# Two recurrent and attention layers with expert retrieval: candidate sums with a PSUM operand, a load buffer that lives longer, and a denser gather pace

## The chip, the cores and the metric

The kernel runs on one core of a Trainium2 chip. The metric is the device time of one execution in microseconds (us). Times of several runs are given as a median. A profiled execution gives the rows quoted below: what each engine did and what it waited for. The engines are PE (matrix products), DVE (vector), ACT (scalar functions), POOL (general work), and SP, which here only issues loads. Each engine runs its instructions in a fixed order.

## The reference

There are 512 tokens of width 1024 and two layers. Each layer is a mixer and an expert layer (PEER), both behind a modulated norm and both added back with a gate. The mixer of layer 0 is a gated linear recurrence (LRU, width 1408), that of layer 1 is causal attention with forget gates. The expert layer has 16384 experts, the pairs of 128 by 128 keys; each of 8 heads picks 16:

```python
def peer_ffn(h, q_w, subkey1, subkey2, expert_u, expert_v):
    ...
        q = (xc @ q_w).reshape(TOKEN_CHUNK, PEER_HEADS, 2, PEER_HALF)
        s1 = jnp.einsum('thd,hnd->thn', q[:, :, 0], subkey1)
        s2 = jnp.einsum('thd,hnd->thn', q[:, :, 1], subkey2)
        v1, i1 = lax.top_k(s1, PEER_TOPK)
        v2, i2 = lax.top_k(s2, PEER_TOPK)
        cand = (v1[..., :, None] + v2[..., None, :]).reshape(...)
        top_s, top_c = lax.top_k(cand, PEER_TOPK)
        ...
        g = jax.nn.softmax(top_s, axis=-1)
        u = jnp.take(expert_u, expert, axis=0)
        act = gelu(jnp.einsum('thkd,td->thk', u, xc))
        w = g * act
        return jnp.einsum('thk,thkd->td', w, jnp.take(expert_v, expert, axis=0))
```

The recurrence is

```python
def rglru_mixer(h, in_w, conv_w, conv_b, ra_w, ra_b, ri_w, ri_b, lam, out_w):
    xb, gb = split(h @ in_w)
    xb = causal_depthwise_conv(xb, conv_w, conv_b)
    r, i = sigmoid(blockdiag(xb, ra_w) + ra_b), sigmoid(blockdiag(xb, ri_w) + ri_b)
    log_a = -8 * softplus(-lam) * r
    u = sqrt(-expm1(2 * log_a)) * (i * xb)
    hs = scan(exp(log_a), u)
    return (hs * gelu(gb)) @ out_w
```

## The kernel before

**Weights.** Products in full precision are made from three products of split operands: high by high, low by high, high by low. A stream object holds all weight blocks in the order of their use. SP loads a block into a buffer `wraw`; ACT copies it to the rounded high half `whi` (line L189); the low half `wlo` = `wraw` - `whi` is made on DVE, or on POOL where `stream.on_pool` is set (L191). There are two load buffers. Where `stream.third` names a pool, every third load goes to a buffer of its own in that pool (L164 to L167), so that three loads can be on their way. A load can start only when the split of the block that was last in its buffer is done.

**Layer 0, in time.** The norm runs to about 46 us, the recurrence (`lru`) to 197, its output projection (`out_proj`, matrix products `oacc` at L599 to L601) to 266. In the recurrence the third buffer is in the pool `lw`, until the last block of input weights, when `third` becomes None. Pool `lw` closes at its end, so that the projection uses the pool `mw` for its third buffer in its first half, and none in its second. The results `yhi`, `ylo` of the recurrence lie in the pool `ly`, which lives to the end of the projection.

**Query stage of the expert layer** (`queries`, 290 to 470 us in layer 0, 1880 to 2060 in layer 1). For each of 8 heads and both halves of a query, PE projects the query into PSUM (`pacc`, L556 to L558), ACT takes the high half `qh` (L953), DVE the low half `ql` = `pacc` - `qh` (L954), and PE makes the scores `sps` against 128 keys (L941 to L943; the last of the three needs `ql`). DVE finds the 16 greatest of each set (`top16`: MAX8, its index, replacement, again), and puts them into `vals[0]` and `vals[1]`. After the first heads, `search` follows, one head behind: it adds the two sets to 50 candidates that can be among the 16 greatest sums, `cand`, by eight adds at L924 and one at L926, for all four blocks of 128 tokens at once, and takes their 16 greatest. In this stage POOL makes the `wlo` and the products `mq` (L264) of modulation matrices with a broadcast condition vector, whose sums ACT takes (L249). Between heads PE also makes the first inner products of the expert loop (`first_up`).

**Expert loop** (`expert_in`, `gated`, `expert_out`; 769 to 1480 us in layer 0, 2333 to 3064 in layer 1). Three of the four blocks of 128 tokens go through all experts, as dense products with gates of which most are zero. The loop runs over 128 chunks of 128 experts. Some chunks have their inner activations stored from an earlier stage ("stored"), the others make them here. DVE multiplies activations `at` by gates (L1331), and makes the low half `wl` (L1339) of the result `wh`, which PE needs for the products `vacc` (L1346). The fourth block of tokens goes another way: beside the loop, POOL gathers for each of its 128 (head, rank) pairs the rows of `expert_u`, later of `expert_v` (L1221), and DVE makes a product with the tokens (`rows`, L1234) and later a weighted sum (`accg`, L1248). These 256 steps are a background generator: in each chunk `pump` gives it a credit, by the two numbers of `PUMP`, the first for chunks that aren't stored, the second for stored ones; a step costs 1.2 of credit. What is left after the loop runs at once in `bg.finish()`.

The order of the instructions of each engine is set by a scheduler that works from its own costs, except for instructions that are pinned with `keep_in_program_order`, among them `wl` and the gathers' vector operations.

Of the kernel before, what the change touches and what calls it, by code (L numbers as in the profile page):

```python
# [6 lines left out]
F32 = mybir.dt.float32  # L7
# [5 lines left out]
AF = mybir.ActivationFunctionType  # L13
# [6 lines left out]
TC = S // 128  # L20
KD = D // 128
DR = 1408
NR = DR // 128
# [5 lines left out]
PH = 8  # L29
PK = 128  # L30
TOPK = 16
# [5 lines left out]
XT = 32  # L37
EARLY = (4, 0, 0, 2, 0, 2, 2, 2)
NEARLY = sum(EARLY)
PUMP = (4.05, 1.31)  # L40
QROWS = 6
LAG = 2
AHEAD = 6
# [633 lines left out]
def lru(g, h, head, conv, bias, lam, during, grow_fn, after):  # L677

    tc, nc = g.tc, g.nc
    V, A = nc.vector, nc.scalar  # L680
    with pool(tc, name="lruy", bufs=1) as ly:
        yhi = ly.tile([128, NR, S], F32R, name="yhi")
        ylo = ly.tile([128, NR, S], F32R, name="ylo")
        with pool(tc, name="lru", bufs=1) as lp, pool(tc, name="lruw", bufs=2) as lw:
            cv = lp.tile([128, NR, 5], F32, name="cv")
            nc.sync.dma_start(cv, conv)
            gb = lp.tile([128, 2, NR], F32, name="gbias")
            nc.sync.dma_start(gb, bias)
            lm = lp.tile([128, NR], F32, name="lm")
            nc.sync.dma_start(lm, lam)  # L690

            def small(name):
                return lp.tile([128, NR], F32, name=name)
            z = small("z")
            V.tensor_scalar(z, lm, -1.0, None, op0=OP.mult)
            az, th, u, u2, sp = small("az"), small("th"), small("u"), small("u2"), small("sp")
            den = small("den")
            A.activation(az, lm, AF.Abs)
            A.activation(th, az, AF.Tanh, scale=0.5)
            V.tensor_scalar(den, th, 3.0, None, op0=OP.add)  # L700
            V.reciprocal(den, den)
            V.tensor_scalar(u, th, -1.0, 1.0, op0=OP.mult, op1=OP.add)
            V.tensor_mul(u, u, den)
            atanh2(g, sp, u, u2)
            V.tensor_scalar(z, z, 0.0, None, op0=OP.max)
            V.tensor_add(sp, sp, z)
            sp2 = small("sp2")
            V.tensor_scalar(sp2, sp, 2.0, None, op0=OP.mult)
            sp4 = small("sp4")
            V.tensor_scalar(sp4, sp, -4.0, None, op0=OP.mult)  # L710
            V.tensor_scalar(gb, gb, 0.5, None, op0=OP.mult)

            psum = g.lps
            with pool(tc, name="lps2", bufs=2, space=PSUM) as psum2:
                g.stream.third = (lw,)
                bg = Background(*during(lw))
                ge = {}
                xc, xh, xl = {}, {}, {}

                def gates(chunks):  # L720


                    sg, T, m = {}, {}, {}
                    for o in chunks:
                        gh, gl = g.stream.take()
                        ins = [i for i in (o - 1, o, o + 1) if 0 <= i < NR]
                        for w in range(2):
                            ps = psum2.tile([128, S], F32, name=f"gps{w}", tag=f"gps{w}")
                            for i in ins:
                                b = i - o + 1  # L730
                                nc.tensor.matmul(ps, gh[:, w, b, :], xh[i], start=(i == ins[0]), stop=False)
                                nc.tensor.matmul(ps, gh[:, w, b, :], xl[i], start=False, stop=False)
                                nc.tensor.matmul(ps, gl[:, w, b, :], xh[i], start=False, stop=(i == ins[-1]))
                            sg[o, w] = lw.tile([128, S], F32, name=f"sg{w}", tag=f"sg{w}")
                            A.activation(sg[o, w], ps, AF.Tanh, scale=0.5, bias=gb[:, w, o:o + 1])
                    for o in chunks:
                        r = sg[o, 0]
                        T[o] = lw.tile([128, S], F32, name="T", tag="T")
                        A.activation(T[o], r, AF.Tanh, scale=sp2[:, o:o + 1], bias=sp2[:, o:o + 1])
                        A.activation(r, r, AF.Exp, scale=sp4[:, o:o + 1], bias=sp4[:, o:o + 1])  # L740
                    for o in chunks:
                        m[o] = lw.tile([128, S], F32, name="m", tag="m")
                        tc.keep_in_program_order(A.activation(m[o], T[o], AF.Sqrt, scale=0.25))
                    for o in chunks:
                        a, i_ = sg[o, 0], sg[o, 1]
                        V.scalar_tensor_tensor(m[o], a, 1.0, m[o], op0=OP.add, op1=OP.mult)
                        V.scalar_tensor_tensor(i_, i_, 1.0, xc[o], op0=OP.add, op1=OP.mult)
                        V.tensor_mul(m[o], m[o], i_)
                        hs = T[o]
                        V.tensor_tensor_scan(hs, a, m[o], 0.0, op0=OP.mult, op1=OP.add)  # L750
                        V.tensor_mul(hs, hs, ge[o])
                        split(g, yhi[:, o, :], ylo[:, o, :], hs)

                for j in range(NR):
                    if j == NR - 1:
                        g.stream.third = None
                    ps = head.pop(0) if head else proj_t(g, psum, h)
                    xp = lw.tile([128, S + 3], F32, name="xp", tag="xp")
                    V.memset(xp[:, 0:3], 0.0)
                    A.activation(xp[:, 3:], ps, AF.Copy)  # L760
                    xc[j] = lw.tile([128, S], F32, name="xc", tag="xc", bufs=4)
                    A.activation(xc[j], ps, AF.Identity, scale=cv[:, j, 3:4], bias=cv[:, j, 4:5])
                    for k in (2, 1, 0):
                        V.scalar_tensor_tensor(xc[j], xp[:, k:k + S], cv[:, j, k:k + 1], xc[j],
                                               op0=OP.mult, op1=OP.add)
                    xh[j] = lw.tile([128, S], F32R, name="xh", tag="xh", bufs=4)
                    xl[j] = lw.tile([128, S], F32R, name="xl", tag="xl", bufs=4)
                    split(g, xh[j], xl[j], xc[j])
                    bg.pump(LP)
                    ps = head.pop(0) if head else proj_t(g, psum, h)  # L770
                    ge[j] = lw.tile([128, S], F32, name="ge", tag="ge", bufs=3)
                    A.activation(ge[j], ps, AF.Gelu)
                    if j and j % 2 == 0:
                        gates((j - 2, j - 1))
                    if j == NR - 2:
                        grow = grow_fn(psum)
                    bg.pump(LP)
                bg.finish()
                gates((NR - 1,))
            g.lguard.__exit__(None, None, None)  # L780
        with pool(tc, name="mw", bufs=2) as mw, pool(tc, name="ops", bufs=1, space=PSUM) as psum:
            out_proj(g, psum, (yhi, ylo), NR, grow, Background(*after(mw)), mw)


def finish_mixer(g, y, nk, grow, after):
# [63 lines left out]
def peer(g, norm_fn, u, v, grow_fn, query_rows, nq, last_rows, nd, cost):  # L849
# [3 lines left out]
    V, A, T = nc.vector, nc.scalar, nc.tensor  # L853
# [6 lines left out]
    with pool(tc, name="pk", bufs=1) as pk:  # L860
# [32 lines left out]
        vals = [rs.tile([128, TC, PH, TOPK], F32, name=f"vals{w}") for w in range(2)]  # L893
# [9 lines left out]
        env = {}  # L903
# [13 lines left out]

        def search(hd):

            v1, v2 = vals[0][:, :, hd], vals[1][:, :, hd]  # L920
            cand = env["qw"].tile([128, TC, NCAND], F32, name="cand", tag="cand", bufs=1)
            for i in range(8):
                n = ROWN[i]
                V.tensor_tensor(cand[:, :, ROWO[i]:ROWO[i] + n], v2[:, :, 0:n],  # L924
                                v1[:, :, i:i + 1].to_broadcast([128, TC, n]), op=OP.add)
            V.tensor_tensor(cand[:, :, ROWO[8]:NCAND], v1[:, :, 8:16],  # L926
                            v2[:, :, 0:1].to_broadcast([128, TC, 8]), op=OP.add)
            for t in range(TC):
                top16(top[:, t, hd, :], pos[:, t, hd, :], cand[:, t, :], NCAND)

        def queries(pw, psum, banks):

            todo = []
            rows = itertools.chain(*query_rows(pw))
            due = 0.0

# [727 lines left out]
def model(tc, *aps):  # L1664
# [4 lines left out]
    with ExitStack() as ctx:  # L1669
# [39 lines left out]
        def flat(n):  # L1709
# [7 lines left out]
        peer(g, normed("l0_ffn"), flat("l0_u"), flat("l0_v"), grow("l0_ffn"),  # L1717
             lambda p: (queried("l0_ffn", p, gate), queried("l1_mix", p, every[AT:])), 30 / 15, None, 3, PUMP)
        fox(g, normed("l1_mix"), *arg("fox_", "fb", "qg", "kg"), lambda p: (mod("l1_ffn", p, first[M1:], 1),),
# [101 lines left out]
```

## Time and profile before

| what | us |
|---|---|
| median of three runs | 3087.73 (3086.15 to 3087.94) |
| profiled execution | 3084.97 |
| its span, first to last instruction | 3083.1 |
| PE busy | 2978.3 |
| DVE busy | 2621.3 |
| ACT busy | 1449.4 |
| POOL busy | 1188.9 |

The span is what the rows cover; the execution's own time is 1.9 us longer. A row of a timeline gives the start, the duration, the engine, the line of the code, the operation, output and inputs, shapes and a count, and in brackets how long the engine had sat idle and which instruction ended that. A row of a table of waits gives the waiting engine and line, whom it waited for, and then total us, number of waits, and the longest. A row of a table of windows gives the stretch, its length, busy us (and number of instructions) of the engines asked for, the granted clock of PE as a share of full speed, the busy share of the DMA engines, and GB/s. A row of a table of groups gives, behind the shapes and the count, busy us in total and the mean in ns.

### The profile page before, as it was taken

The numbers are of one execution on the slowest core, as the hardware profiler recorded it, in microseconds if no ns is written. First come the engines' busy times: TensorE is split into PE (matmuls) and PEld (weight loads), VectorE is DVE, ScalarE is ACT, GpSimd is POOL, SyncE is SP. The second block draws the span as 40 slices with busy tenths as digits, with TensorE's granted clock in tenths as the row PEclk, the third lists the DMA queues.
The fourth block names the chain that finished last, engine by engine and source line by source line (L and its number), as shares of the span: only waits on it lengthen the run. The fifth ranks groups of instructions, "written<-read, shape, count | busy, mean of one in ns | idle before, by whom it ended". The sixth has DMA issues, their size and how long they took to land.

```text
span 3083.1 us, 44436 instructions
## 1 busy us (share of the span) xinstructions
PE 2978.3 (97%) x16232; PEld 2616.2 (85%) x16232; DVE 2621.3 (85%) x4951; ACT 1449.4 (47%) x2284; POOL 1188.9 (39%) x906
## 2 busy tenths in 40 slices
PE   8999889999999999999999999899999999999998
PEld 6778679999888888888787778799999888888887
DVE  7866999997788889888869877989996888888888
ACT  6655445566333333333448844355564333333332
POOL 1002764110556555555211002542203755565552
PEclk9999889999999999999999999999999999999999
DMA  7445446798999999998542144358998999999996
GB/s 295 172 179 181 160 154 256 284 313 287 358 376 367 370 370 384 360 372 318 219 139 79 50 157 155 111 177 314 337 292 314 393 354 375 382 372 355 364 365 238
DMA packets 306844, 855.23 MB, mean 277 GB/s; under 512 B 26208, under 2 KB 161408, under 8 KB 267840
## 3 DMA queue, kind: packets, MB, share of 16 engines
q1 hardware_dynamic: 72464, 407.65, 34.7%
q0 software_dynamic: 93440, 336.11, 28.9%
q10 hardware_dynamic: 140720, 108.63, 10.8%
q8 instruction: 127, 2.08, 0.2%
q14 instruction: 93, 0.76, 0.1%
HBM read 767.93 MB, written 83.51 MB: 276 GB/s over the span
## 4 chain that ended last, share of the span: by engine, by line
PE 64%; DVE 21%; issue 7%; ACT 5%; DMA 3%; POOL 0%; DVEq 0%; SPq 0%; ACTq 0%; POOLq 0%
PE vacc L1346 25%; PE pacc L556 10%; PE pacc L558 10%; PE pacc L557 10%; DVE accg L1248 2%; DVE cand L924 2%; PE gps L1178 2%; ACT whi L189 2%; DVE wlo L191 2%; DVE pg L1205 1%; DVE tk L899 1%; DVE wl L1339 1%; DMA wraw<-in_l_vp_dram 1%; DVE idxs L898 1%; DVE idxs L901 1%
## 5 line engine op out<-in xcount | busy, mean ns | idle before, releaser
L189 ACT ACTIVATE whi<-wraw 128x1024 fp32r<-128x1024 f32 (+1 forms) x646 | 669.5, 1039 | 1023.6 <-PE vacc L1346 397.1
L191 DVE TENSOR_TENSOR wlo<-wraw,whi 128x1024 fp32r<-128x1024 f32 (+2 forms) x580 | 699.7, 1217 | 331.7 <-ACT whi L189 331.3
L556 PE MATMUL pacc<-hhi,whi 128*128 128x352 f32 (+1 forms) x2600 | 895.7, 345 | 0.0
L558 PE MATMUL pacc<-hhi,wlo 128*128 128x352 f32 (+1 forms) x2600 | 887.0, 341 | 1.7 <-DVE wlo L191 1.6
L557 PE MATMUL pacc<-hlo,whi 128*128 128x352 f32 (+1 forms) x2600 | 887.1, 341 | 0.0
L1346 PE MATMUL vacc<-whi,wh 128*128 128x512 f32 x1536 | 598.9, 390 | 0.0
L1346 PE MATMUL vacc<-wlo,wh 128*128 128x512 f32 x1536 | 597.9, 389 | 0.0
L1346 PE MATMUL vacc<-whi,wl 128*128 128x512 f32 x1536 | 553.8, 395 | 12.6 <-DVE wl L1339 11.7
L1221 POOL DMA_INDIRECT rows<-in_l_v_dram,ei x256 | 391.4, 1529 | 328.1 <-DVE accg L1248 278.2
L557 PEld LDWEIGHTS pacc<-hlo,whi 128*128 128x128 f32 x2600 | 495.3, 191 | 26.6
L556 PEld LDWEIGHTS pacc<-hhi,whi 128*128 128x128 f32 x2600 | 494.0, 190 | 27.2
L1221 POOL DMA_INDIRECT rows<-in_l_u_dram,ei x256 | 416.4, 1627 | 259.9 <-DVE rows L1234 196.1
L558 PEld LDWEIGHTS pacc<-hhi,wlo 128*128 128x128 f32 x2600 | 493.3, 190 | 27.0 <-DVE wlo L191 2.8
L1346 PEld LDWEIGHTS vacc<-whi,wl 128*128 128x128 f32 x1536 | 282.5, 188 | 91.5 <-DVE wl L1339 34.3
L1346 PEld LDWEIGHTS vacc<-whi,wh 128*128 128x128 f32 x1536 | 288.3, 188 | 57.1 <-ACT wh L1334 0.6
L1346 PEld LDWEIGHTS vacc<-wlo,wh 128*128 128x128 f32 x1536 | 288.7, 188 | 56.1
L1248 DVE SCALAR_TENSOR_TENSOR accg<-rows,act,accg 128x1024 f32<-128x1024 f32 x254 | 325.7, 1282 | 2.9
L1234 DVE SCALAR_TENSOR_TENSOR rows<-rows,hn 128x1024 f32<-128x1024 f32 x256 | 302.1, 1222 | 0.1
L1334 ACT ACTIVATE wh<-at 128x768 fp32r<-128x768 f32 x128 | 108.4, 847 | 240.2 <-DVE at L1331 235.4
L191 POOL TENSOR_TENSOR wlo<-wraw,whi 128x1024 fp32r<-128x1024 f32 (+1 forms) x62 | 125.2, 2027 | 139.3 <-ACT whi L189 139.2
L1083 POOL DMA_INDIRECT rowx<-in_l_u_dram,eix x36 | 61.0, 1695 | 242.5 <-DVE rowx L1101 153.4
L1331 DVE TENSOR_TENSOR at<-at,gtile 128x768 f32<-128x768 f32 x128 | 122.2, 954 | 0.0
(342 smaller groups left out, 3757.6 us busy)
## 6 DMA issues: line engine op xcount, KB each, us to landing
wraw<-in_l_uT_dram SPq DMA_DIRECT2D x128, 1024.0 KB, 8.0
wraw<-in_l_vp_dram SPq DMA_DIRECT2D x128, 1024.0 KB, 8.6
gscr<-st ACTq DMA_DIRECT2D x48, 1024.0 KB, 6.8
gtile<-gscr SPq DMA_DIRECT2D x90, 512.0 KB, 7.3
ascr<-at ACTq DMA_DIRECT2D x136, 176.0 KB, 4.7
at<-ascr ACTq DMA_DIRECT2D x68, 352.0 KB, 8.4
mw<-in_l_ffn_mw_dram POOLq DMA_DIRECT2D x32, 512.0 KB, 4.1
wraw<-in_l_qw_dram SPq DMA_DIRECT2D x16, 1024.0 KB, 4.8
```

The lines of the kernel that those rows point to most:

```text
L189: self.pin(nc.scalar.activation(hi, raw, AF.Copy))
L191: self.pin((nc.gpsimd if self.on_pool else nc.vector).tensor_sub(lo, raw, hi))
L556: nc.tensor.matmul(ps, whi[:, k, :], hhi[:, k, :n], start=(k == 0), stop=False))
L557: nc.tensor.matmul(ps, whi[:, k, :], hlo[:, k, :n], start=False, stop=False)
L558: nc.tensor.matmul(ps, wlo[:, k, :], hhi[:, k, :n], start=False, stop=(k == KD - 1))
L924: V.tensor_tensor(cand[:, :, ROWO[i]:ROWO[i] + n], v2[:, :, 0:n], v1[:, :, i:i + 1].to_broadcast([128, TC, n]), op=OP.add)
L1221: i = nc.gpsimd.indirect_dma_start(out=rows, out_offset=None, in_=src, in_offset=bass.IndirectOffsetOnAxis(ap=ei[:, j:j + 1], axis=0))
L1234: V.scalar_tensor_tensor(r, r, 1.0, hn, op0=OP.mult, op1=OP.mult, accum_out=act[:, j:j + 1]))
L1248: i = V.scalar_tensor_tensor(acc, r, w, acc, op0=OP.mult, op1=OP.add)
L1331: pin(V.tensor_tensor(shp, shp, gts[c // 8][:, :, c % 8:c % 8 + 2, :].rearrange("p b c t -> p c b t"), op=OP.mult))
L1334: (pin if c < 2 else lambda x: x)(A.activation(wh, at, AF.Copy))
L1346: T.matmul(acc[t][d], x[:, ts], y[:, d, :], start=(i == 0 and x is wh and y is vh), stop=(i == PK - 1 and x is wl))
```

## The change

Three edits. The pace numbers of the gathers rise by some 3%. In the recurrence the third load buffer is in pool `ly` and stays in use to its end and through the first half of the output projection. In `search`, ACT copies a head's `vals[0]` into a PSUM tile `v1`, which takes the bank of the tag "tp" (otherwise used for transposes), and the nine adds on DVE read that operand from there.

```diff
-PUMP = (4.05, 1.31)
+PUMP = (4.15, 1.35)
...
-                g.stream.third = (lw,)
+                g.stream.third = (ly,)
...
                 for j in range(NR):
-                    if j == NR - 1:
-                        g.stream.third = None
...
         with pool(tc, name="mw", bufs=2) as mw, pool(tc, name="ops", bufs=1, space=PSUM) as psum:
-            out_proj(g, psum, (yhi, ylo), NR, grow, Background(*after(mw)), mw)
+            out_proj(g, psum, (yhi, ylo), NR, grow, Background(*after(mw)), ly)
...
         def search(hd):
 
-            v1, v2 = vals[0][:, :, hd], vals[1][:, :, hd]
+            v2 = vals[1][:, :, hd]
+            v1 = env["v1"][:, :, hd * TOPK:(hd + 1) * TOPK]
+            A.activation(v1, vals[0][:, :, hd], AF.Copy)
             cand = env["qw"].tile([128, TC, NCAND], F32, name="cand", tag="cand", bufs=1)
             for i in range(8):
                 n = ROWN[i]
...
         def queries(pw, psum, banks):
 
             todo = []
+            env["v1"] = psum.tile([128, TC, PH * TOPK], F32, name="v1", tag="tp", bufs=1)
```

Lines from the search on move by one or two (L954 becomes L955, L1248 becomes L1249, L1339 becomes L1340; `top16` moves up by two).

DVE, layer 0, the sums of head 0, before (`vals_2603` is the first set, `vals_2604` the second; both are in SBUF):

```order
L899 MATCH_REPLACE tk<-vals_2604,sps 128x128
L924 TENSOR_TENSOR cand<-vals_2604,vals_2603 128x4x8
L924 TENSOR_TENSOR cand<-vals_2604,vals_2603 128x4x5
L900 MAX vals_2604<-tk 128x8
L924 TENSOR_TENSOR cand<-vals_2604,vals_2603 128x4x4
L924 TENSOR_TENSOR cand<-vals_2604,vals_2603 128x4x3
L901 MAX_INDEX idxs_2606<-vals_2604,tk 128x8
L924 TENSOR_TENSOR cand<-vals_2604,vals_2603 128x4x16
L924 TENSOR_TENSOR cand<-vals_2604,vals_2603 128x4x2 x3
L926 TENSOR_TENSOR cand<-vals_2603,vals_2604 128x4x8
```

The same place now (`v_2618` is the tile in PSUM):

```order
L898 MAX vals_2604<-tk 128x8
L899 MAX_INDEX idxs_2606<-vals_2604,tk 128x8
L924 TENSOR_TENSOR cand<-vals_2604,v_2618 128x4x16
L924 TENSOR_TENSOR cand<-vals_2604,v_2618 128x4x8
L924 TENSOR_TENSOR cand<-vals_2604,v_2618 128x4x5
L924 TENSOR_TENSOR cand<-vals_2604,v_2618 128x4x4
L924 TENSOR_TENSOR cand<-vals_2604,v_2618 128x4x3
L924 TENSOR_TENSOR cand<-vals_2604,v_2618 128x4x2 x3
L955 TENSOR_TENSOR ql<-pacc,qh 128x512
L926 TENSOR_TENSOR cand<-v_2618,vals_2604 128x4x8
```

The adds now stand together behind the last search of the second set, and the next `ql` has moved up between them. On ACT, the first copy stands just ahead of the high half of a block of query weights, in layer 0, where there was nothing between the rows around it:

```order
L249 ACTIVATE mq,qdot<-mq 128x1024
L253 ACTIVATE gate_l_ffn<-qdot,bias_l_ffn 128x1
L920 ACTIVATE v_2618<-vals_2603 128x4x16
L189 ACTIVATE whi<-wraw 128x1024
L954 ACTIVATE qh<-pacc 128x512
```

SP, the loads of the recurrence's output projection, before:

```order
L173 DMA wraw_1778<-in_lru_out_dram 128x2048
L173 DMA wraw_1860<-in_lru_out_dram 128x2048
L173 DMA wraw_1952<-in_lru_out_dram 128x1024
L173 DMA wraw_1982<-in_lru_out_dram 128x512
L173 DMA wraw_2046<-in_lru_out_dram 128x2048
L173 DMA wraw_2012<-in_lru_out_dram 128x2048
L173 DMA wraw_2152<-in_lru_out_dram 128x1024
```

and now:

```order
L173 DMA wraw_1778<-in_lru_out_dram 128x2048
L173 DMA wraw_1860<-in_lru_out_dram 128x2048
L173 DMA wraw_1952<-in_lru_out_dram 128x1024
L173 DMA wraw_1982<-in_lru_out_dram 128x512
L173 DMA wraw_2012<-in_lru_out_dram 128x2048
L173 DMA wraw_2046<-in_lru_out_dram 128x2048
L173 DMA wraw_2152<-in_lru_out_dram 128x1024
```

Blocks are used in the order of their numbers. The fifth, `wraw_2012`, was issued behind the sixth; now it stands ahead of it, and its buffer is the one of the second, `wraw_1860`.

DVE, the end of layer 1's expert loop, before:

```order
L1331 TENSOR_TENSOR at_29267<-at_29267,gtile 128x768
L1248 SCALAR_TENSOR_TENSOR accg<-rows,act,accg 128x1024
L191 TENSOR_TENSOR wlo<-wraw,whi 128x1024
L1248 SCALAR_TENSOR_TENSOR accg<-rows,act,accg 128x1024 x3
L1339 TENSOR_TENSOR wl<-at_29267,wh 128x768
L1331 TENSOR_TENSOR at_29339<-at_29339,gtile 128x768
L191 TENSOR_TENSOR wlo<-wraw,whi 128x1024
L1339 TENSOR_TENSOR wl<-at_29339,wh 128x768
```

and now:

```order
L1249 SCALAR_TENSOR_TENSOR accg<-rows,act,accg 128x1024 x2
L191 TENSOR_TENSOR wlo<-wraw,whi 128x1024
L1340 TENSOR_TENSOR wl<-at_29182,wh 128x768
L1332 TENSOR_TENSOR at_29303<-at_29303,gtile 128x768
L191 TENSOR_TENSOR wlo<-wraw,whi 128x1024 x2
L1340 TENSOR_TENSOR wl<-at_29303,wh 128x768
L1332 TENSOR_TENSOR at_29375<-at_29375,gtile 128x768
L1340 TENSOR_TENSOR wl<-at_29375,wh 128x768
```

The last gathered sums (`accg`) now come two pairs of chunks earlier.

## The prediction

> **What bounds the kernel now.** I read the page's busy shares first, then PE's waits stage by stage, and then the timelines of the engines named there.
>
> ```profile
> PE 2978.3 (97%) x16232; PEld 2616.2 (85%) x16232; DVE 2621.3 (85%) x4951; ACT 1449.4 (47%) x2284; POOL 1188.9 (39%) x906
> ```
>
> PE is busy for 97% of 3083.1 us, so about 105 us of idle time is all that shorter waits can return, and beside it the time in which PE ran at a lower granted clock. The change touches four stages. PE's waits in them are, in this order: the query stage of layer 0 (290 to 470 us) and of layer 1 (1880 to 2060), the LRU output projection (two rows, 197 to 270), the expert loop of layer 0 with its end (770 to 1520), the same loop without its end (770 to 1465), and the loop of layer 1 (2333 to 3083).
>
> ```profile
> PE sps L943 <- DVE ql L954: 28.8, 7, 9.8
> PE sps L943 <- DVE ql L954: 9.6, 4, 5.6
> PE oacc L599 <- ACT whi L189: 4.0, 1, 4.0
> PE oacc L600 <- DVE wlo L191: 0.5, 1, 0.5
> PE vacc L1346 <- DVE wl L1339: 6.3, 8, 3.1
> PE vacc L1346 <- DVE wl L1339: 2.4, 5, 1.3
> PE vacc L1346 <- DVE wl L1339: 5.5, 8, 3.1
> ```
>
> The query stage of layer 0 is the costliest: seven waits, 28.8 us, all for ql, the low half of a query, which DVE makes in order behind its search work.
>
> **Candidate sums.** These are the busy times of line L924's adds in the two query stages, then a window of all engines, then DVE's adds of one head (three rows), POOL's operations beside them (three rows), and one ql with the POOL operation that ran across it.
>
> ```profile
> 280.00:470.00 190.00, 53.37 (x56) 0.90 0.48 175
> 1880.00:2060.00 180.00, 19.96 (x64) 0.98 0.38 135
> 310.00:470.00 160.00, 131.16 (x656) 117.47 (x655) 151.53 (x731) 67.20 (x123) 113.69 (x94) 0.88 0.41 150
> ```
> ```profile
> 351.50 3.99 DVE L924 TENSOR_TENSOR cand<-vals,vals 128x32 f32<-128x32 f32 x2
> ...
> 355.61 2.25 DVE L924 TENSOR_TENSOR cand<-vals,vals 128x16 f32<-128x16 f32 x2
> ...
> 358.06 0.43 DVE L924 TENSOR_TENSOR cand<-vals,vals 128x64 f32<-128x64 f32 x4
> ```
> ```profile
> 348.40 2.40 POOL L191 TENSOR_TENSOR wlo<-wraw,whi 128x1024 fp32r<-128x1024 f32 x1 [0.71 <-ACT whi L189]
> 350.76 4.69 POOL L264 TENSOR_TENSOR mq<-mq,sc 128x1024 f32<-128x1024 f32 x2
> 355.40 2.34 POOL L191 TENSOR_TENSOR wlo<-wraw,whi 128x1024 fp32r<-128x1024 f32 x1
> ```
> ```profile
> 345.26 2.43 POOL L191 TENSOR_TENSOR wlo<-wraw,whi 128x1024 fp32r<-128x1024 f32 x1
> ...
> 346.50 0.67 DVE L954 TENSOR_TENSOR ql<-pacc,qh 128x512 fp32r<-128x512 f32 x1
> ```
>
> An add of 16 to 32 elements took up to two microseconds while POOL worked: the pair begun at 351.50 ended at 355.49 where POOL's pair ended (350.76 + 4.69 = 355.45), and the next pair ended at 357.86, where POOL's next operation ended at 357.74. With POOL idle four adds took 0.43 us. So an add with two SBUF operands waits out POOL's operations. The ql at 346.50 reads one operand from PSUM, lay wholly inside a POOL operation, and took 0.67 us. I take it that an add with one PSUM operand escapes in the same way.
>
> Eight free adds of L924 cost 2 x 0.43 = 0.86 us a head. Layer 0 pays 53.37 - 7 x 0.86 = 47.3 us too much on DVE (seven heads' adds fall into the window), layer 1 19.96 - 8 x 0.86 = 13.1 us. What PE gets back is less, since PE waits only in part of that time. In layer 0, between 310 and 470 us, PE idles 160 - 131.16 = 28.8 us, and in its busy time the mean granted clock was 0.88, so its work at the full clock is about 131.16 x 0.88 = 115.4 us. The upper end is therefore 160 - 115.4 = 44.6 us. POOL's 113.69 us and DVE's 151.53 - 47.3 = 104.2 us both fit under that time, but hardly: each is near PE, and POOL is as good as full. Those seven waits include two long ones:
>
> ```profile
> 360.58 0.47 PE L943 MATMUL sps<-whi,ql 128*128 128x128 f32 x1 [7.83 <-DVE ql L954]
> 410.87 0.48 PE L943 MATMUL sps<-whi,ql 128*128 128x128 f32 x1 [9.82 <-DVE ql L954]
> ```
>
> The lower end is these two alone, 17.7 us, with the shorter waits staying because POOL takes their place. I take 28, the idle time as such: the clock is then given back only where a new small wait doesn't take it again. In layer 1, PE's waits are 9.6 us and DVE's excess 13.1; the ends are 5.6 (the longest wait alone goes) and 13; I take 9.
>
> The copy to PSUM costs ACT eight instructions a layer. Nearest rows in this stage are a one-element ACTIVATE, and the wait that gives ACT room:
>
> ```profile
> L253 ACT ACTIVATE gate_l_ffn<-qdot,bias_l_ffn 128x1 f32<-128x1 f32 x8 | 2.3, 291 | 0.2
> ACT whi L189 <- PE pacc L557: 76.2, 23, 6.2
> ```
>
> At 0.3 us each that is 2.4 us a layer, under 76.2 us of ACT's idle time in layer 0: nothing on the path, and 2.4 us if that cover were gone. The copy waits for DVE's first set of top values and stands in ACT's order ahead of a whi; the adds come only after the second set, half a head later, so DVE should find it done. What DVE itself pays for a PSUM operand is bounded by two rows of the same operation and size, one reading PSUM (sps), one SBUF (tk):
>
> ```profile
> L897 DVE MAX8 vals<-sps 128x8 f32<-128x128 f32 x64 | 18.7, 291 | 7.1 <-PE sps L943 7.1
> L900 DVE MAX8 vals<-tk 128x8 f32<-128x128 f32 x63 | 17.7, 281 | 0.2
> ```
>
> The difference is 10 ns, or 9 x 8 x 0.01 = 0.7 us a layer on DVE, which I put at nothing, since DVE gains 47. The Trainium skill's "VectorE: DVE Perf Modes", in its section on the errata, speaks against the change here: it gives a DVE instruction 58 cycles of fixed cost with an SBUF source and 120 with a PSUM source, at 0.96 GHz. By it, my estimate is 62 cycles or 65 ns more for each add, 4.7 us of DVE time a layer, and some 4 us less gain in layer 0; the two rows above show 10 ns where it says 65, so I go by the rows.
>
> **Third weight buffer.** After the LRU's gates, its third load buffer was in a pool that closes; the fifth block of the output projection's weights used one of the next pool. Now the buffer lives on, and that load stands ahead of its neighbour in SP's order. Rows: DVE's split of the block three earlier, SP's issue, ACT's split of the block, and PE around it.
>
> ```profile
> 210.53 1.22 DVE L191 TENSOR_TENSOR wlo<-wraw,whi 128x1024 fp32r<-128x1024 f32 x1
> ```
> ```profile
> 218.25 0.81 SPq L173 DMA_DIRECT2D wraw<-in_lru_out_dram  x2
> ```
> ```profile
> 230.65 2.95 ACT L189 ACTIVATE whi<-wraw 128x1024 fp32r<-128x1024 f32 x3 [12.38 <-DMA wraw<-in_lru_out_dram]
> ```
> ```profile
> 227.34 0.40 PE L601 MATMUL oacc<-whi,ylo 128*128 128x512 f32 x1
> 231.76 0.80 PE L599 MATMUL oacc<-whi,yhi 128*128 128x512 f32 x1 [4.03 <-ACT whi L189]
> 233.02 0.80 PE L600 MATMUL oacc<-wlo,yhi 128*128 128x512 f32 x1 [0.47 <-DVE wlo L191]
> ...
> 238.10 0.39 PE L600 MATMUL oacc<-wlo,yhi 128*128 128x512 f32 x1
> ```
>
> The load was issued at 218.25, behind one that had to wait for its buffer, and landed just before 230.65, 12 us later. In the changed order it needs the buffer of the block three earlier, whose split ends at 211.75, and stands first: it lands by about 224 even if it takes 12 us again, ahead of PE's need at 227.7. Both waits go (4.0 and 0.5), and so does the slow clock behind them. From 227.34 to 238.10 PE issued 14 matmuls; at the pitch of 0.23 us in the full clock it needs 14 x 0.23 = 3.2 instead of 10.8. That is 7.5 us; the lower end is the 4.5 of the waits. I take 7. Earlier loads move up by one block too, and ACT meets the first output block's split ahead of the last gates' work, which can cost the LRU's tail up to 1.5 us; this stands in the range. The longer-lived buffer also makes three small loads at the LRU's start wait for earlier work, behind which PE has its first block of input weights: nothing, or about 1 us uncovered.
>
> **Gather pacing.** Each chunk of the loop now admits 4.15 instead of 4.05 (1.35 instead of 1.31 when stored) of gather work. By my count from the code 256 steps at 1.2 need 307.2; before, the loop admits about 305.2, and the rest falls to its very end, after about 313.2, so that the last gathers come some five steps earlier. DVE at the end of layer 1's loop, where accg is the gathers' sum and wl what PE waits for:
>
> ```profile
> 3059.35 3.92 DVE L1248 SCALAR_TENSOR_TENSOR accg<-rows,act,accg 128x1024 f32<-128x1024 f32 x3
> 3063.19 0.95 DVE L1339 TENSOR_TENSOR wl<-at,wh 128x768 fp32r<-128x768 f32 x1
> ```
> ```profile
> PE vacc L1346 <- DVE wl L1339: 3.8, 3, 3.1
> ```
>
> The second fence is PE's waits from 3030 us to the end, and the loop of layer 0 gives the same row from 1465 to 1520. In the changed order no accg stands between the last three wl, so these 3.8 us a layer go: 7.6 at most. Against it each chunk carries 2.5 to 3% more gather work, on DMA engines that are already full in parts of the loop:
>
> ```profile
> 1310.00:1340.00 30.00, 26.05 (x24) 1.00 1.01 412
> ```
>
> (stretch, its length, DVE busy, clock, DMA share, GB/s). The waits within the loops, 2.4 us in layer 0 and 5.5 - 3.8 = 1.7 in layer 1, could double: then the pacing is worth 7.6 - 4.1 = 3.5. As the lower end I put a stop of 0.1 us in each of 120 pairs of chunks (60 in a loop), 7.6 - 12 = -4.4. I take 6.
>
> **The sum.** 28 + 9 + 7 + 6 = 50 us off the profiled execution, whose time was 3084.97 us: 3035. The median of the runs, 3087.73, stands 2.8 above it, so the forecast against the median is 3037.7, which I give as 3038. The stages that follow each gain keep PE over 97% busy, so an earlier start carries through.
>
> **Rivals.** (1) POOL takes DVE's place in layer 0. For it: 113.69 us of work in a stage that would last 132, where the weight halves for PE queue behind pairs of mq operations.
>
> ```profile
> L264 POOL TENSOR_TENSOR mq<-mq,sc 128x1024 f32<-128x1024 f32 x27 | 64.0, 2395 | 0.0
> L191 POOL TENSOR_TENSOR wlo<-wraw,whi 128x1024 fp32r<-128x1024 f32 (+1 forms) x31 | 62.5, 2023 | 54.6 <-ACT whi L189 54.5
> ```
>
> If one mq of 2.4 us delays a wlo in each of eight heads, 19 of the 28 us are lost: gain 9 + 9 + 7 + 6 = 31, 3057. Against it: POOL today waits 54.5 us for ACT in that stage, so it runs ahead, and would have to lose all of that. (2) The adds are not freed by a PSUM operand: what lets ql through is something else. Then only 7 + 6 = 13 remain: 3075. The trace has no two-operand add of this small size from PSUM. (3) On the other side of no change: the copy blocks ACT. It waits for DVE's values and holds the whi behind it, and so POOL's wlo and PE. At head 0 the last of those values and that whi were these:
>
> ```profile
> 303.25 0.29 DVE L900 MAX8 vals<-tk 128x8 f32<-128x128 f32 x1
> 304.02 1.06 ACT L189 ACTIVATE whi<-wraw 128x1024 fp32r<-128x1024 f32 x1 [4.57 <-PE pacc L557]
> ```
>
> There were 0.5 us of slack. Where DVE is late, PE is then late through both ql and whi. It decides against the change from 50/16 = 3.1 us lost for each of 16 heads; at 5 us (a whole set of top values) it is 80 lost against 50: 3118. Against it: DVE loses 60 us of work and so is seldom late. (4) The pacing stops PE in the loops, at its lower end: 28 + 9 + 7 - 4.4 = 39.6, 3048.
>
> **Chances.** Forecast 0.63, with a range of its own from 3024 to 3050; POOL 0.18; adds not freed 0.08; copy blocks ACT 0.05; pacing 0.06. All ends at their best give 44.6 + 13 + 7.5 + 7.6 = 72.7, 3015; all at their worst 17.7 + 5.6 + 4.5 - 1.5 - 4.4 = 21.9, 3066. I start the range at 3019 and end it at 3064, past POOL's case, which leaves out the second and third rivals (0.13) and little below. A measurement tells some 0.2%, 6 us, from no change. Slower by more: rival three, 0.04. Within: part of two and three, 0.03. Faster: 0.93.
>
> **What would show it.** Right: the adds in layer 0's query stage together near 7 us instead of 53, with POOL busy beside them; PE's wait for ql there under 8 us; POOL's own waits for ACT well under 54; no wait for whi in the LRU's output projection and a clock of 1.00 through it; no wait for wl in the last three pairs of chunks of either loop. Wrong: adds that still end where POOL's operations end; PE waiting for wlo from POOL, or ACT's copy waiting while a whi stands behind it; more than 5 us of waits for wl inside a loop. The prediction as a whole fails if the query stage of layer 0 keeps its length.

## The result, and the profile after

The changed kernel took 3040.52 us in the median of four runs (3037.91 to 3042.44), the kernel before 3087.84 (four runs, the three given above among them): a ratio of 0.9845, 95% interval 0.9828 to 0.9862. The forecast was 3038, range 3019 to 3064. The profiled execution's span is 3040.4 us.

First the page's busy shares, then PE's waits by stage. Stages now begin earlier, and lines have moved by one: query stage of layer 0 (280 to 470 us) and of layer 1 (1840 to 2030), output projection (197 to 270), expert loop of layer 0 with its end (740 to 1500) and of layer 1 (2290 to 3043).

```profile
PE 2964.9 (98%) x16232; PEld 2605.4 (86%) x16232; DVE 2563.0 (84%) x4951; ACT 1451.8 (48%) x2300; POOL 1157.9 (38%) x906
```
```profile
PE sps L944 <- DVE ql L955: 0.7, 1, 0.7
PE sps L944 <- DVE ql L955: 0.7, 1, 0.7
PE oacc L600 <- DVE wlo L191: 0.7, 1, 0.7
PE vacc L1347 <- DVE wl L1340: 10.4, 6, 3.0
PE vacc L1347 <- DVE wl L1340: 10.9, 7, 2.7
```

The waits for ql have gone (28.8 and 9.6 before), those of the output projection are down from 4.5 to 0.7, but the waits for wl in the loops have risen, from 6.3 to 10.4 and from 5.5 to 10.9.

Where the 43 us came from is read off the first matrix products of the stages, in the two profiled executions. Each length is from the first row of one output on PE to the first of the next (the last loop: to its last product):

| stage | before | changed | difference |
|---|---|---|---|
| to the output projection | 196.8 | 198.5 | +1.7 |
| output projection | 69.1 | 62.6 | -6.5 |
| first scores to the next stage, layer 0 | 195.7 | 153.1 | -42.6 |
| expert loop, layer 0 | 745.4 | 753.6 | +8.2 |
| first scores to the next stage, layer 1 | 165.3 | 153.2 | -12.1 |
| expert loop, layer 1 | 744.9 | 753.7 | +8.8 |
| all other stages together | 961.0 | 960.7 | -0.3 |

**Sums.** The busy times of L924 in the two query stages, and the window of all engines in layer 0's stage (PE, PE's weight loads, DVE, ACT, POOL, clock, DMA):

```profile
270.00:440.00 170.00, 6.39 (x64) 1.00 0.63 226
1840.00:2000.00 160.00, 6.38 (x64) 1.00 0.41 145
```
```profile
306.50:432.00 125.50, 124.80 (x706) 112.96 (x706) 112.24 (x790) 73.35 (x136) 113.09 (x100) 1.00 0.57 207
```

The adds take 6.4 us in place of 53.4 and 20.0. PE is busy for 124.80 of 125.50 us, at the full clock, where it was busy for 131.16 of 160 at 0.88. POOL's 113.09 us of work fit into it with little to spare. DVE's adds of head 0, and POOL at the same time:

```profile
306.50 0.76 DVE L924 TENSOR_TENSOR cand<-vals,v 128x64 f32<-128x64 f32 x8
```
```profile
302.67 4.75 POOL L264 TENSOR_TENSOR mq<-mq,sc 128x1024 f32<-128x1024 f32 x2
307.38 3.11 POOL L191 TENSOR_TENSOR wlo<-wraw,whi 128x1024 fp32r<-128x1024 f32 x2
```

Eight adds ran in 0.76 us, wholly inside POOL's pair of operations, which ended only at 307.42. Of the 72 adds of a layer none took more than 0.21 us. The price of the PSUM operand is read from the ninth add, L926, in the views of the tile cand, of before and of the changed kernel (minimum, median, maximum in ns):

```profile
L926 DVE TENSOR_TENSOR cand<-vals,vals x7: 178/179/184, 320.2 to 454.1; 128x32 f32<-128x32 f32 x7
```
```profile
L926 DVE TENSOR_TENSOR cand<-v,vals x8: 179/183/185, 307.8 to 427.9; 128x32 f32<-128x32 f32 x8
```

That is 4 ns, not the 65 worked out from the errata table of the Trainium skill's page "VectorE: DVE Perf Modes".

**Load.** SP issued the fifth block at 213.72 us, where it had been 218.63 (the second issue of the row that begins at 218.25), and PE's window over the place of the old stop is full, at the full clock (before: 10.51 of 15 us and 0.87 from 220 to 235):

```profile
222.00:237.00 15.00, 15.00 (x65) 1.00 0.61 217
```

**Loops.** The stop at the loop's end has gone, and stops inside have come. DVE ahead of one of them, in the changed kernel, and at the same place before:

```profile
1240.41 3.92 DVE L1249 SCALAR_TENSOR_TENSOR accg<-rows,act,accg 128x1024 f32<-128x1024 f32 x3
1244.24 1.22 DVE L191 TENSOR_TENSOR wlo<-wraw,whi 128x1024 fp32r<-128x1024 f32 x1
1245.38 1.32 DVE L1249 SCALAR_TENSOR_TENSOR accg<-rows,act,accg 128x1024 f32<-128x1024 f32 x1
1246.62 0.94 DVE L1340 TENSOR_TENSOR wl<-at,wh 128x768 fp32r<-128x768 f32 x1
```
```profile
1287.64 3.92 DVE L1248 SCALAR_TENSOR_TENSOR accg<-rows,act,accg 128x1024 f32<-128x1024 f32 x3
1291.48 0.95 DVE L1339 TENSOR_TENSOR wl<-at,wh 128x768 fp32r<-128x768 f32 x1
```

One more sum (1.3 us) and a low half of a weight (1.2) now stand ahead of wl, and PE, which had waited 0.37 us here (the last row below, of before), waits 3.02 and then runs slowly:

```profile
1247.62 1.84 PE L1347 MATMUL vacc<-whi,wl 128*128 128x512 f32 x6 [3.02 <-DVE wl L1340]
1249.25 0.63 PE L1347 MATMUL vacc<-whi,wh 128*128 128x512 f32 x1
```
```profile
1292.48 1.65 PE L1346 MATMUL vacc<-whi,wl 128*128 128x512 f32 x6 [0.37 <-DVE wl L1339]
```

In the changed kernel, stops of 2.7 to 3.0 us stand at 1247.6, 1357.7 and 1443.4 us, and at 2808.2, 2918.3 and 3003.8. Behind each of these six some products ran at 0.63 us in place of 0.39, which cost about 1.5 us more a stop. So of the 17 us that the two loops lost, about 10 are longer waits (21.3 us for wl over the span, 11.7 before), and the slow products make up the rest.

### The profile page after: what moved, and what is told of

It reads as the page before. It is cut to its first block, busy times and chain, and to the rows that moved or that the text cites. A ratio compares the mean times of both kernels' runs of the same rounds, so it can differ in the third digit from the quotient of the medians.

```text
span 3040.4 us, 44431 instructions
## 1 busy us (share of the span) xinstructions
PE 2964.9 (98%) x16232; PEld 2605.4 (86%) x16232; DVE 2563.0 (84%) x4951; ACT 1451.8 (48%) x2300; POOL 1157.9 (38%) x906
## 4 chain that ended last, share of the span: by engine, by line
PE 69%; DVE 16%; issue 8%; ACT 4%; DMA 2%; POOL 1%; DVEq 0%; ACTq 0%; SPq 0%; POOLq 0%
PE vacc L1347 27%; PE pacc L556 11%; PE pacc L557 10%; PE pacc L558 10%; DVE accg L1249 2%; PE gps L1179 2%; DVE wlo L191 2%; ACT whi L189 1%; DVE pg L1206 1%; DVE rows L1235 1%; DVE wl L1340 1%; PE oacc L600 1%; PE oacc L599 1%; PE oacc L601 1%; DMA wraw<-in_l_uT_dram 1%
## 5 line engine op out<-in xcount | busy, mean ns | idle before, releaser
L1347 PE MATMUL vacc<-whi,wl 128*128 128x512 f32 x1536 | 564.3, 399 | 22.0 <-DVE wl L1340 21.3
L1222 POOL DMA_INDIRECT rows<-in_l_v_dram,ei x256 | 369.6, 1444 | 348.0 <-DVE accg L1249 275.2
L1222 POOL DMA_INDIRECT rows<-in_l_u_dram,ei x256 | 409.3, 1599 | 242.7 <-DVE rows L1235 179.3
L1249 DVE SCALAR_TENSOR_TENSOR accg<-rows,act,accg 128x1024 f32<-128x1024 f32 x254 | 326.3, 1285 | 3.1
L1340 DVE TENSOR_TENSOR wl<-at,wh 128x768 fp32r<-128x768 f32 x128 | 121.8, 951 | 1.8 <-ACT wh L1335 1.8
```

The costliest lines, as they stand in the source:

```text
L1222: i = nc.gpsimd.indirect_dma_start(out=rows, out_offset=None, in_=src, in_offset=bass.IndirectOffsetOnAxis(ap=ei[:, j:j + 1], axis=0))
L1249: i = V.scalar_tensor_tensor(acc, r, w, acc, op0=OP.mult, op1=OP.add)
L1340: return lambda: pin(V.tensor_sub(wl, at, wh))
L1347: T.matmul(acc[t][d], x[:, ts], y[:, d, :], start=(i == 0 and x is wh and y is vh), stop=(i == PK - 1 and x is wl))
```

## The experiments

Three questions: does each part do what the stages say; is it the PSUM operand that frees the sums; and why does a denser pace cost time. On the last, theory P says that position matters. Two chunks that share one wl are called a pair here. From the two pace numbers the steps can be counted that `pump` admits in each chunk. PE makes inner products for some of the later chunks; at the pairs 7, 16, 25, 34, 43, 52 and 59 of the loop it makes none for two pairs running, so it needs the next wl soonest there. Ahead of that wl stand the last steps of the pair before and the first of this one: by the old pace 1 + 3 at all seven, by the new one 1 + 4 at 43, 52 and 59, which are the three stops. At 25 and 34 it has 2 + 3, also five, with no stop at 25 and 0.24 us at 34: the four in the last chunk before the wl are what hurts. Rival D says that density matters: more gather work at a time overloads DVE or the DMA engines.

**The old pace, with sums and load buffer as changed**

```diff
-PUMP = (4.15, 1.35)
+PUMP = (4.05, 1.31)
```

> The change with the old pace numbers (4.05, 1.31): sums from PSUM and the longer-lived load buffer alone. Theory P (the new pace costs time, because it puts one more gather step ahead of a low half wl where PE is shortest): both expert loops return to their old length, 745 us instead of 754, so the time is about 3040.5 - 17 = 3024. Rival T (the loops are longer because they now start earlier or in another phase, not because of the pace): the loops stay at 754 and the time at 3040.

Measured: 3028.48 us, ratio 0.9817 (0.9799 to 0.9835). The loops took 749.5 and 744.9 us; the profile's span was 3023.4. PE's waits over the whole span, with the stops of 3.1 us back at both ends:

```profile
PE vacc L1347 <- DVE wl L1340: 13.1, 17, 3.1
```

So the new pace cost about 12 us in the median. By the two ratios it is 9 us, with intervals that overlap a little (0.9828 to 0.9862 and 0.9799 to 0.9835), so this pair of runs alone would not settle it; the run of the pace alone, below, does. The loop of layer 0 was 4 us longer than before for two reasons. It had three waits of 0.9 to 1.3 us in its first half, where the kernel before had one of 1.3. And behind the stop of 3.08 us at its end the products ran at 0.63 us, which cost some 2.6 us, where in the kernel before they ran at 0.39 behind the same stop.

**The sums alone** (the kernel before with only the copy and the adds as changed)

> The kernel before with the PSUM operand of the sums alone. Layer 0's query stage, from its first scores to the next stage, should shorten by 42 to 43 us and layer 1's by 12, as in the changed kernel's trace, so 3088 - 55 = 3033; my prediction's sizes of 28 and 9 would give 3051. PE's wait for wl should be as before, 3 us at each loop's end.

Measured: 3036.47 us, ratio 0.9842 (0.9824 to 0.9859); query stages 153.1 and 153.2 us, as in the changed kernel. The output projection keeps its stop and its length (69.9 us):

```profile
PE oacc L599 <- ACT whi L189: 4.4, 1, 4.4
```

**The pace alone** (the kernel before with `PUMP = (4.15, 1.35)`)

> The kernel before with the new pace numbers alone. Theory P: each loop gains its 3.1 us stop at the end and loses three stops of 2.7 to 3 us with slow clock behind each, +8 us a loop, 3104. My prediction's step: 6 us less, 3082. Rival T (an interaction with the earlier start): no change, 3088.

Measured: 3100.86 us, ratio 1.0055 (1.0035 to 1.0075). The loops took 754.2 and 750.4 us; PE waited for wl, over the whole span,

```profile
PE vacc L1346 <- DVE wl L1339: 20.6, 14, 2.7
```

where it had waited 11.7 us before, with three stops of 2.7 us in each loop. The earlier start isn't needed for it: the pace alone makes the kernel slower. The loop of layer 1 lost 3 to 4 us less than that of layer 0 because two of its stops had no slow products behind them:

```profile
2865.36 1.65 PE L1346 MATMUL vacc<-whi,wl 128*128 128x512 f32 x6 [2.74 <-DVE wl L1339]
2866.85 0.39 PE L1346 MATMUL vacc<-whi,wh 128*128 128x512 f32 x1
```

**Load buffer alone**

> The kernel before with the longer-lived load buffer alone. The output projection goes from 69 to 62.5 us, as in the changed kernel, and 3088 becomes 3081. If the recurrence pays for the buffer, its end moves from 196.8 to 198.5 us and 3083 is left; the runs without this edit, whose recurrence ended at 198.0 and 198.8, speak against that.

Measured: 3080.56 us, ratio 0.9984 (0.9973 to 0.9996); the output projection took 61.6 us. The recurrence ended at 198.8 us, but so it did in the run of the pace alone, without this edit. The +1.7 us of the table above is therefore no measure of the buffer's cost: the recurrence ended between 196.8 and 198.8 us in the four traces without the edit and between 197.6 and 199.1 in the eight with it. A cost of about a microsecond can't be excluded.

**ACT's copy into SBUF instead of PSUM**

```diff
-            env["v1"] = psum.tile([128, TC, PH * TOPK], F32, name="v1", tag="tp", bufs=1)
+            env["v1"] = pw.tile([128, TC, PH * TOPK], F32, name="v1", tag="v1", bufs=1)
```

> As the run with the old pace, but ACT's copy of the first set of values goes to a tile in SBUF instead of PSUM: same instructions, both operands of the sums in SBUF. Theory S (what frees the sums is that one operand is in PSUM): the sums in layer 0's query stage take some 50 us again, the stage goes from 153 back to 190 to 196 us, layer 1's from 153 to 165, and the time from 3028 to 3080. Rival R (the order of DVE, or the fresh copy, freed them): sums at 7 us, 3028.

Measured: 3104.83 us, ratio 1.0053 (1.0036 to 1.007), with the load buffer's gain in it. L924's busy time in the query stages, and the longest waits of PE (whole span) and of ACT (280 to 480 us):

```profile
280.00:480.00 200.00, 64.23 (x64) 0.88 0.46 164
1840.00:2100.00 260.00, 27.34 (x64) 0.94 0.40 145
```
```profile
PE sps L944 <- DVE ql L955: 52.0, 10, 13.0
```
```profile
ACT v L920 <- DVE vals L898: 63.9, 6, 15.6
```

The sums are long again with the same copy, so the fresh copy isn't what freed them. DVE's order changed in this run too: the adds stand between the searches again, as in the kernel before. So this run alone doesn't part the operand's place from the order; the next one does. The stages took 205.5 and 175.9 us, 10 longer than before the change. Where DVE is late, the copy waits in ACT's queue (63.9 us, against 24.8 in the changed kernel), with the high halves of PE's weights behind it: the mechanism of my third rival. That it makes the 10 us wasn't tested apart.

**POOL's products narrow, in the kernel before**

```diff
-        pin(P.tensor_tensor(wf, wf, g.sc, op=OP.mult))
+        pin(P.tensor_tensor(wf[:, :64], wf[:, :64], g.sc[:, :64], op=OP.mult))
```

> The kernel before, with POOL's products mq done for 64 of 1024 columns only (the modulation loses the rest): these POOL operations fall from 2.4 us to about 0.2, and half of POOL's work in layer 0's query stage goes. Theory S (the sums wait for whatever POOL operation with two SBUF operands is under way): the sums go from 53 us to about 25, what the weight halves on POOL block, the stage from 196 to about 165 and the time to about 3055. Rival R (the sums are long for a reason of their own): 53 us and 3088.

Measured: 3044.41 us, ratio 0.9854 (0.984 to 0.987). The sums, with both operands in SBUF, in the two stages:

```profile
280.00:480.00 200.00, 14.01 (x64) 0.98 0.60 216
1840.00:2100.00 260.00, 7.96 (x64) 0.98 0.56 207
```

From 53.4 us (56 adds) to 14.0 (64 adds), with DVE's instructions in the same order as in the kernel before: the sums had waited for POOL, and the order isn't what made them long. Together with the run before it this leaves the operand's place as what frees them. The adds that are still long end where one of POOL's `wlo` operations ends. That the total is less than the 25 expected may mean that the pairs of mq did most of the blocking, or only that POOL now has gaps, so that fewer adds meet one of its operations; the run doesn't part these. The stages took 157.9 and 155.7 us.

**Same credit as the new pace, steps placed otherwise**

```diff
-PUMP = (4.05, 1.31)
+PUMP = (4.12, 1.39)
```

> Sums and load buffer as changed, pace (4.12, 1.39): in sum the same credit as the new pace (320 against 319 over a loop) but such that before no low half wl of the pairs of chunks 25, 34, 43, 52 and 59, where PE is short, more than four gathered steps fall. Theory P (position): no stop of 2.7 us in the loops and none of 3 us at their end, loops of about 741 us, 3040.5 - 24 = 3017. Rival D (density: more gather work at a time costs DVE or the DMA engines): loops of 754 again, 3040.

Measured: 3017.57 us, ratio 0.9775 (0.9756 to 0.9795); loops of 743.4 and 740.9 us. The stops at the loops' ends are gone and none of 2.7 us has come. PE's wait for wl over the whole span, the longest of 1.9 us:

```profile
PE vacc L1347 <- DVE wl L1340: 5.7, 13, 1.9
```

Before that one of 1.9 us DVE had itself waited 1.3 and 0.5 us for gathered rows. Another execution of the same kernel (below, 739.9 and 740.0 us) has no wait for wl over 0.4 us. A late row can thus make a single stop that another execution doesn't have.

**More credit still, placed so too**

```diff
-PUMP = (4.05, 1.31)
+PUMP = (4.35, 1.32)
```

> Sums and load buffer as changed, pace (4.35, 1.32): more credit than the new pace (328 against 319 over a loop), again with no more than four gathered steps before the wl of the pairs where PE is short. Theory P (position): loops of 741 to 743 us, 3016, as with (4.12, 1.39). Rival D (density): worse than (4.12, 1.39) by some us a loop, 3025 or more.

Measured: 3017.64 us, ratio 0.977 (0.9753 to 0.9786); loops of 741.6 and 741.8 us. Some 3% more credit than the changed kernel's pace cost nothing where the steps lie well.

**One hundredth, placed badly** (beside the fastest version on the same chip)

```diff
-PUMP = (4.05, 1.31)
+PUMP = (4.05, 1.32)
```

> Sums and load buffer as changed, pace (4.05, 1.32): one hundredth on the second number of the old pace, credit 311.3 against 310.6 over a loop, but by the count of steps five instead of four fall before the wl of the pairs 7 to 59 where PE is short. Theory P (position): stops of 2.7 to 3 us at pairs 43, 52 and 59, with slow clock behind each, in both loops, as with the pace (4.15, 1.35), while the stop of 3.1 us at the end shrinks; loops of 752 to 756 us and 3040. Rival D (density): loops of 745 to 748, 3028.

> The fastest version beside the one before it on the same chip: 3017 to 3018 again, and ahead of the pace (4.05, 1.32) by 22 us by theory P, by 10 or less by rival D.

Measured: 3056.67 us (ratio 0.9896, 0.9878 to 0.9914) against 3015.35 (0.9767, 0.9751 to 0.9784). The loops took 763.1 and 758.8 us, against 739.9 and 740.0:

```profile
PE vacc L1347 <- DVE wl L1340: 33.5, 19, 4.0
```

With 1 + 4 steps at all seven pairs there are seven stops of over a microsecond in layer 0's loop, 106 to 110 us apart but for the last (821.9, 930.2, 1036.9, 1145.3, 1255.4, 1365.4 and 1452.0), of 1.1 to 4.0 us, and seven in layer 1's. The kernel was 41 us behind the fastest version, where theory P had said 22 and rival D 10 or less. The loss was larger than theory P's own figure, at least in part because it named three stops of the seven. That position makes these stops is shown: with a credit of 311 for a loop they come, with 320 and 328 they don't, so density isn't their cause over this range.

Over all twelve traces the loops fall into groups by pace: 744.9 to 749.5 us by the old one (12 loops), 750.4 to 754.2 by the new one (4), 739.9 to 743.4 by the two that place the steps well (6), and 758.8 and 763.1 by (4.05, 1.32).

## Why the prediction was right, point by point

The time fell into the range, 2.5 us from the forecast, but by two errors that cancelled: the sums gave 18 us more than forecast, and the pacing 23 less. That the forecast came so close is luck; its mechanisms for the sums and the load buffer were right, that for the pacing was wrong.

- **Sums, layer 0: mechanism right, size too small.** "I take 28, the idle time as such: the clock is then given back only where a new small wait doesn't take it again." Measured: 42.6, near the upper end of 44.6. The waits fell to 0.7 us, so no small wait took the clock again, and it was 1.00 all through. Both experiments on the mechanism (copy in SBUF, narrow products) bear out its step "an add with two SBUF operands waits out POOL's operations".
- **POOL's own waits for ACT** fell from 54.5 to 9.0 us in layer 0's query stage, as the prediction asked.
- **Sums, layer 1:** 9 taken, 12.1 measured, within the ends of 5.6 and 13.
- **The copy on ACT** cost PE nothing: eight of 228 ns in layer 0. But ACT waited 24.8 us for DVE's values in eight waits, the longest 7.0, with other work behind the copy in its order. The prediction names such waits as a sign of being wrong; here they did no harm, since PE was busy all through.
- **Load buffer:** 7 taken, 6.5 measured in the stage; alone, the ratio's interval gives 1 to 8 us. The load was issued at 213.72, two microseconds later than the prediction had it, still in time. The doubt about the recurrence's tail (1.5 us) is neither borne out nor excluded.
- **Gather pacing: the step that failed.** "I take 6" of gain; measured are 17 us of loss by the stages, 14 in the run of this edit alone (3100.86 - 3087.08) and 12 between the old and the new pace with the rest as changed (3040.52 - 3028.48). The gain at the loop's end was real, the 3.1 us stop is gone. But I looked for the cost in the amount, "2.5 to 3% more gather work", spread over 120 pairs as a stop of 0.1 us each. It lies in three pairs a loop, 2.7 to 3.0 us each, with slow products behind it. Even my lower end, -4.4, was too mild, and the prediction's sign of being wrong, over 5 us of waits for wl inside a loop, came in both (10.4 and 10.9). The count of steps by chunk could have been made beforehand from the two numbers.
- **Count of credit.** "and the rest falls to its very end" was wrong: the loop admits 310.6 of credit by the old pace and 318.8 by the new, not 305.2 and 313.2, so all 256 steps are admitted inside it at the old pace too. What stood ahead of the last wl was the last pairs' own steps, 3 + 2.
- **Rivals.** POOL did become the busiest beside PE (20.00 of 20 us in some windows), but PE ran at 20.00 beside it:

```profile
350.00:370.00 20.00, 20.00 (x106) 17.04 (x104) 18.33 (x131) 14.32 (x27) 20.00 (x22) 1.00 0.60 225
```

  The pacing rival, given 0.06, is what happened, hidden in the total by the larger gain of the sums.

## What to carry to other kernels

Where a vector engine's small operations show a few durations that are ten times their least, look at what another engine ended at the same moment; here moving one operand to PSUM took 53 us of such operations down to 6. When idle time comes with a lower granted clock, the gain of removing it is bounded by both, and it may reach that bound if the waits go altogether. When background work is paced by credits, count which steps fall ahead of the instruction that the main engine needs soonest, at the places where that engine has least work; a hundredth in a pace number moved this kernel by 28 us (3056.67 against 3028.48, from runs on two occasions; 24 by the ratios), and the pace (4.12, 1.39) beats the changed kernel by some 23 us (also from two occasions).

## What the runs showed that I had not expected

- A stop of 2.7 to 3.1 us on PE can cost half as much again, or nothing more. After the stop at 1247.6 us seven rows ran at 0.63 us in place of 0.39, and the granted clock of that 40 us window was 0.96; all six long stops of the changed kernel's profile went so. Of the six in the run of the pace alone, two didn't (2865.4 and 2973.9 us, clock 1.00 from 2850 to 2890), and the two of 3.08 us at the loops' ends in the kernel before didn't either, while seven of the twelve stops of 3.1 us at loop ends in all traces did. So the length of a stop alone doesn't decide it, and the same kernel can differ by some us a loop between executions. Waits of 0.2 to 0.4 us left no such trace: before, the windows around stops of 0.37 us show 1.00. The Trainium skill's "TensorE: Matmul & The Clock Gate" (Part 1, what's actually happening) has the clock fall after an idle window of about 3.4 us; here stops shorter than that were followed by the slow products, so the measurement differs.
- The operand in PSUM that frees the vector engine costs little to put there: ACT pays 228 ns for a copy of 64 elements into PSUM and 256 into SBUF (246 to 258), so the copy is no dearer for its place.

What stays open: why waits of about 1 to 2 us stand in one execution and not in another in the loops' first half (three in layer 0 in the run with the old pace, one in the kernel before), and what decides whether slow products follow a stop.
